# 98 transposes in pairs on the halves of the array, and the mLSTM's state products by head

## Chip, cores and metric

The kernel runs on one core of a Trainium2 chip. The metric is the device time of one execution in microseconds (us). The kernel before takes 916.1 us (median of 3 runs, 916.0 to 916.24); a change of about 0.2% (1.8 us) is what a measurement of this kernel can tell from no change.

## The reference

One decoder layer on x of 512 tokens by 1024 features, all float32: half a step of a gated FFN, a token mixer with two groups of heads, and a second FFN, each between RMS norms.

```python
x = x + 0.5 * rms_norm(swiglu_ffn(rms_norm(x, norm_pre[0]), ffn1_w_in, ffn1_w_out), norm_post[0])
x = x + rms_norm(token_mixer(rms_norm(x, norm_pre[1]), w_mix_in, ...), norm_post[1])
x = x + 0.5 * rms_norm(swiglu_ffn(rms_norm(x, norm_pre[2]), ffn2_w_in, ffn2_w_out), norm_post[2])

def swiglu_ffn(x, w_in, w_out):            # D_FF = 2816
    gate, up = split(x @ w_in, 2)
    return (silu(gate) * up) @ w_out

# token_mixer: one projection h @ w_mix_in gives all heads their inputs
#   HGRN2, 4 heads of 128:   S_t = diag(f_t) S_{t-1} + (1 - f_t) v_t^T,  o_t = S_t^T q_t
#   mLSTM, 4 heads, q and k of 64, v of 128:
#       num = inter * q.C + P.v,   den = inter * q.n + sum(P),   h = num / max(|den|, exp(-m))
#       C, n: a running state of k v^T and of k, decayed by the gates
#   each head normed and gated, both groups side by side, then @ w_mix_out
```

## The kernel before

**Products.** TensorE multiplies in float32r, with every operand as a high part and a low part, three products for one (`mm3`, lines 198 to 200; `prod`, line 619; `in_k`, line 549). So whatever is a factor is first "split": ScalarE casts the high part (line 370 for activations, 294 and 299 for weights), VectorE subtracts it from the source to get the low part (lines 371, 296, 302). `xq[0..3]` hold the activations in this form, features on the partitions: index 2c+h is token half c (256 tokens) and feature half h.

**Transposes.** Activations come with tokens on the partitions, so each tile i of 128 tokens is turned: `turn` (line 364) makes four 128x128 transposes into one PSUM bank, by a product with an identity as the moving operand and the tile as the weights. The bank is then evicted by one cast and one subtraction. `to_t` does this for both feature halves, `to_s` for tiles 0 and 1 of the second FFN (`part`, lines 384 and 386, which also keeps a copy, line 388), `hgrn_edges` for decayed keys of HGRN2 (line 1403), `mlstm_scores` for the keys of the mLSTM (line 1672). There are 146 such transposes; 48 at the head of both FFNs (`start`, `sums`) have no part in the change.

**mLSTM values.** `mlstm_values(c)` runs for the four chunks of 128 tokens. For each pair p of heads it takes a PSUM bank, multiplies the queries of both heads (2 x 64 rows) with a state `C` that is block diagonal (258 columns, zeros off the blocks; line 1739), and adds for each head P times v (line 1742, 129 columns: 128 values and the denominator). ScalarE squares from the bank (line 1747), VectorE and GpSimd work out a factor, VectorE writes the result (line 1761), and with that the bank is free. `chunks` runs three such chunks in a staggered way and fills in with `fill`, pieces of a running projection (lines 198 to 200).

**Order.** Each engine runs its instructions in one fixed order. Most of it is the order of the program text as the framework's scheduler rearranges it when the kernel is built; PSUM is a ring of eight banks, and a bank is handed out again when its last reader is done. Around the change: in `mix_out0` (the output projection's left half) all four tiles of the HGRN2 half of `y` are turned first and the first half of the products follows, then the mLSTM half tile by tile. In the second FFN's head (`ffn_head`), after the last product of the right half (`last`), product p1 (line 619, 24 matmuls over both token tiles 0 and 1: eight with high parts, eight with the low part of the activations, eight with the low part of the weights) starts at once.

Of the kernel before, what the change touches and what calls it, by code (L numbers as in the profile page):

```python
# [11 lines left out]
ALU = mybir.AluOpType  # L12
# [111 lines left out]
class Layer:  # L124
    def __init__(self, ctx, tc, aps):
        self.tc, self.nc = tc, tc.nc
        self.__dict__.update(aps)
        nc = self.nc
        pool = lambda name, **kw: ctx.enter_context(tc.tile_pool(name=name, bufs=1, **kw))
        self.cp, self.wp, self.sp, self.psp = pool("cp"), pool("wp"), pool("sp"), pool("psp", space=PSUM)  # L130
        self.uid, self.hold = 0, ()
        self.wt, self.free, self.slot = None, deque(), {}

        self.ident = self.cp.tile([P, P], F32, name="ident")
        make_identity(nc, self.ident)
# [4 lines left out]
        xq = {n: self.cp.tile([P, 2 * D + 2 * STEP * (n == 0)], F32R, name=f"xq{n}") for n in (1, 2, 3, 0)}  # L140
        self.xt = [xq[n] for n in range(4)]
        self.xq = [t[:, : 2 * D].rearrange("p (b k t) -> p b k t", b=2, k=KH) for t in self.xt]

        x0 = self.xt[0].rearrange("p (b x) -> p b x", b=2)[:, :, :D].rearrange("p b (k t) -> p b k t", k=KH)
        self.xh = [x0, *self.xq[1:]]
        self.prm = self.cp.tile([P, 36], F32, name="prm")
        self.dram = dram = ctx.enter_context(tc.tile_pool(name="sums", bufs=1, space=bass.MemoryType.DRAM))
        self.sums_of = {
            (f, h, k2): dram.tile([P, 4, QUARTER], F32, name=f"{f}sums{h}_{k2}")
            for f in ("f1", "f2") for h in range(2) for k2 in OUT[f][h] if k2 in QUARTERED[f][h]  # L150
        }
# [212 lines left out]
            self.nc.tensor.transpose(pt[:, c * P : (c + 1) * P], src[:, k * P : (k + 1) * P], self.ident)  # L364
        return pt.rearrange("p (c t) -> p c t", c=4)

    def two(self, dst, i, src):

        v = slice((i % 2) * P, (i % 2 + 1) * P)
        self.nc.scalar.copy(dst[:, 0, :, v], src)  # L370
        self.low = self.nc.vector.tensor_tensor(dst[:, 1, :, v], src, dst[:, 0, :, v].bitcast(F32), op=ALU.subtract)

    def to_t(self, i, src, halves=(0, 1)):

        for h in halves:
            self.two(self.xq[2 * (i // 2) + h], i, self.turn(src, h))

    def part(self, i, h, src):

        pv = self.turn(src, h)  # L380
        v = slice(i * P, (i + 1) * P)
        dst = self.xh[h][:, :, :, v]
        yield
        self.nc.scalar.copy(dst[:, 0], pv)
        yield
        self.nc.vector.tensor_tensor(dst[:, 1], pv, dst[:, 0].bitcast(F32), op=ALU.subtract)
        yield
        self.nc.scalar.copy(self.xf[h][:, :, v], pv)
        yield

    def sums(self, i, src):
# [1003 lines left out]
    def hgrn_edges(self, p, d):  # L1395

        nc = self.nc
        qd = self.qd[:, 2 * p : 2 * p + 2, :]
        nc.vector.tensor_tensor(qd, self.q[p][:, :, P:], qd, op=ALU.mult)
        for a in range(2):  # L1400
            pt = self.ps()
            for c in range(NT - 1):
                nc.tensor.transpose(pt[:, c * P : (c + 1) * P], d[:, a, c * P : (c + 1) * P], self.ident)
            nc.scalar.copy(self.kdt[:, 2 * p + a, :], pt[:, : 3 * P])

    def hgrn_level(self, p, n, ke):

# [229 lines left out]
    def mlstm_scores(self, mc):  # L1637
# [31 lines left out]
        turned = [self.ps() for _ in range(2)]  # L1669
        for p, pt in enumerate(turned):  # L1670
            for c in range(3):
                nc.tensor.transpose(pt[:, c * P : (c + 1) * P], self.qk[:, 2 + p, c * P : (c + 1) * P], self.ident)
        for p in range(2):
            wp = self.col(8)[:, :6]
            nc.vector.tensor_copy(wp.rearrange("p (c a) -> p c a", a=2), w[:, :3, 2 * p : 2 * p + 2])
            nc.vector.tensor_tensor(
                self.kw[:, p].rearrange("p c (a d) -> p (c a) d", a=2),
                turned[p][:, : 3 * P].rearrange("p (n d) -> p n d", d=64),
                wp[:, :, None].broadcast_to([P, 6, 64]),
                op=ALU.mult,  # L1680
            )
# [49 lines left out]
    def mlstm_values(self, c):  # L1731

        nc = self.nc
        s = slice(c * P, (c + 1) * P)
        pm = []
        for p in range(2):
            ps = self.ps()
            if c:
                nc.tensor.matmul(ps[:, :258], self.qdm[:, p, (c - 1) * P : c * P], self.C[:, p, c - 1, :], start=True, stop=False)  # L1739
            for a in range(2):  # L1740
                o = ps[:, 129 * a : 129 * a + 129]
                nc.tensor.matmul(o, self.pT[:, 2 * p + a, s], self.vm[:, c, 2 * p + a, :], start=c == 0, stop=c == 0 or a == 1)  # L1742
            pm.append(ps[:, :258].rearrange("p (a v) -> p a v", a=2))
        sq = self.sp.tile([P, 512], F32, tag="junk", bufs=1, name=self.nm("sq"))
        den, ab, ss, r = self.col(4), self.col(4), self.col(4), self.col(4)
        for p in range(2):
            nc.scalar.activation(sq[:, 256 * p : 256 * p + 256].rearrange("p (a v) -> p a v", a=2), pm[p][:, :, :P], AF.Square)
        yield
        for p in range(2):
            nc.vector.tensor_copy(den[:, 2 * p : 2 * p + 2].rearrange("p (a o) -> p a o", o=1), pm[p][:, :, P : P + 1])  # L1750
# [6 lines left out]
        f = self.rpow(ss, 1.0 / P, EPS)  # L1757
        nc.gpsimd.tensor_tensor(f, f, r, op=ALU.mult)
        yield
        for p in range(2):  # L1760
            nc.vector.tensor_tensor(
                self.y[:, c, W + 256 * p : W + 256 * p + 256].rearrange("p (a v) -> p a v", a=2),
                pm[p][:, :, :P],
                f[:, 2 * p : 2 * p + 2].rearrange("p (a o) -> p a o", o=1).broadcast_to([P, 2, P]),
                op=ALU.mult,
            )
        yield

    def chunks(self, make, n):
# [8 lines left out]
    def mixer(self):  # L1778
# [3 lines left out]
        with tc.tile_pool(name="ma", bufs=1) as ma:  # L1782
# [35 lines left out]
            with tc.tile_pool(name="mc", bufs=1) as mc:  # L1818
# [28 lines left out]
    def mix_out0(self):  # L1847
# [130 lines left out]
```

## Time and profile before

| | us |
|---|---|
| median of 3 runs | 916.1 (916.0 to 916.24) |
| the profiled execution | 916.13 |
| its span in the profile | 914.4 |
| mean granted TensorE clock | 0.999 of full speed |
| VectorE busy | 767.2 |
| ScalarE busy | 522.0 |
| GpSimd busy | 183.7 |

How to read it: times are us from the span's start. A row of the timeline has start, duration, engine, line, operation, output and inputs, shapes, and the count of instructions in the row. The duration of a matmul holds a modelled tail, so one starts long before the record of the one before it ends; the step is what counts, the distance from start to start. A matmul whose duration is longer than that of its like was issued early and waited by the difference. PEld is the loading of weights, which runs beside the matmul before it. Products of plain float32 are recorded as two passes.

### The profile page before, as it was taken

The page shows a single profiled execution, that of the slowest core. Times are in us where ns is not written, and L with a number is a line of the kernel's source. Part 1 is how long each engine was busy: PE and PEld are TensorE (multiplying, and loading weights), DVE is VectorE, ACT ScalarE, POOL GpSimd, SP SyncE. Part 2 cuts the span into 40 slices and gives each one's busy share as a digit, 9 for nine tenths or more (in the row PEclk, how much of TensorE's full clock was granted, in tenths as well). Part 3 has the DMA queues.
Part 4 walks back from the last instruction along what each step waited for, and adds up shares of the span by engine and source line. Part 5 has one row for each costly group of instructions (what it writes and reads, how often), then busy time and mean ns, then how long its engine had stood idle before and what let it go on. Part 6 is the DMA issues. An engine that isn't in the chain of part 4 may idle for free.

```text
span 914.4 us, 18150 instructions
## 1 busy us (share of the span) xinstructions
PE 906.1 (99%) x7330; PEld 874.9 (96%) x7330; DVE 767.2 (84%) x1005; ACT 522.0 (57%) x749; POOL 183.7 (20%) x256
## 2 busy tenths in 40 slices
PE   9999999999999999999999999999999999999997
PEld 8999999999999999998888887899999999999997
DVE  6899988889888876799896556799999889998886
ACT  7645545557566567957643345684454545757661
POOL 2541112121111047742230300322000000010002
PEclk9999999999999999999999999999999999999999
DMA  9355779775897815898953126253344445378542
GB/s 306 88 165 136 189 188 216 187 159 138 219 280 233 258 55 144 162 192 207 214 112 109 47 70 213 65 161 102 97 148 139 138 123 159 104 231 246 170 146 93
DMA packets 127921, 146.51 MB, mean 160 GB/s; under 512 B 16335, under 2 KB 100303, under 8 KB 127837
## 3 DMA queue, kind: packets, MB, share of 16 engines
q1 hardware_dynamic: 111868, 130.14, 46.4%
q0 software_dynamic: 15680, 14.69, 11.9%
q8 instruction: 57, 0.93, 0.4%
q10 hardware_dynamic: 288, 0.52, 0.2%
q14 instruction: 28, 0.22, 0.1%
HBM read 143.20 MB, written 31.48 MB: 191 GB/s over the span
## 4 chain that ended last, share of the span: by engine, by line
PE 62%; ACT 0%; DVE 0%; DVEq 0%; POOLq 0%; issue 0%; POOL 0%; ACTq 0%
PE ps L619 23%; PE ps L1012 8%; PE ps L549 6%; PE ps L198 5%; PE ps L200 5%; PE ps L199 5%; PE ps L1004 4%; PE ps L560 1%; PE ps L1441 1%; PE ps L364 1%; PE ps L1540 0%; PE ps L1742 0%; PE ps L1491 0%; PE ps L1715 0%; PE ps L1739 0%; PE ps L1717 0%
## 5 line engine op out<-in xcount | busy, mean ns | idle before, releaser
L294 ACT CAST w<-raw 128x1024 fp32r<-128x1024 f32 x246 | 250.6, 1027 | 192.0 <-PE ps L619 91.1
L296 DVE TENSOR_TENSOR w<-raw,w 128x1024 fp32r<-128x1024 f32 x246 | 299.4, 1221 | 30.3 <-ACT w L294 28.9
L619 PE MATMUL ps<-xq,w 128*128 128x256 f32 x2016 | 237.4, 277 | 0.0
L619 PEld LDWEIGHTS ps<-xq,w 128*128 128x128 f32 x2016 | 233.3, 188 | 0.1
L619 PE MATMUL ps<-sq,w 128*128 128x256 f32 x1512 | 178.0, 276 | 0.0
L619 PEld LDWEIGHTS ps<-sq,w 128*128 128x128 f32 x1512 | 174.6, 188 | 0.0
L310 DVE TENSOR_TENSOR raw<-raw,raw 128x1024 f32<-128x1024 f32 x72 | 89.7, 1252 | 7.5 <-DMA raw<-in_ffn_w_in_dram 6.2
L1012 PE MATMUL ps<-w,hs 128*128 128x256 f32 x672 | 80.9, 276 | 0.0
L1004 PE MATMUL ps<-w,hs 128*128 128x256 f32 x672 | 79.2, 276 | 0.0
L1012 PEld LDWEIGHTS ps<-w,hs 128*128 128x128 f32 x672 | 78.3, 188 | 0.0
L1004 PEld LDWEIGHTS ps<-w,hs 128*128 128x128 f32 x672 | 77.5, 188 | 0.0
L198 PE MATMUL ps<-w,xq 128*128 128x512 f32 x176 | 71.1, 405 | 0.1
L199 PE MATMUL ps<-w,xq 128*128 128x512 f32 x176 | 68.6, 391 | 0.0
L200 PE MATMUL ps<-w,xq 128*128 128x512 f32 x176 | 68.6, 391 | 0.0
L549 PE MATMUL ps<-xq,w 128*128 128x256 f32 x480 | 55.7, 277 | 0.0
L944 POOL DMA_DIRECT2D f2sums<-in_ffn_w_out_dram x15 | 20.0, 1507 | 177.5 <-DMA f2sums<-in_ffn_w_out_dram 177.0
L549 PEld LDWEIGHTS ps<-xq,w 128*128 128x128 f32 x480 | 54.9, 188 | 0.5 <-issue 0.5
L884 ACT CAST hs<-hf 128x1024 fp32r<-128x1024 f32 x32 | 33.7, 1054 | 28.0 <-PE ps L1012 20.3
L885 DVE TENSOR_TENSOR hs<-hf,hs 128x1024 fp32r<-128x1024 f32 x32 | 39.1, 1223 | 9.0 <-ACT hs L884 8.4
L944 POOL DMA_DIRECT2D f1sums<-f1sums x26 | 22.3, 859 | 110.1 <-DMA f1sums<-in_ffn_w_out_dram 56.1
L944 POOL DMA_DIRECT2D f2sums<-f2sums x30 | 26.3, 905 | 87.1 <-DMA f2sums<-in_ffn_w_out_dram 42.4
L310 POOL TENSOR_TENSOR raw<-raw,raw 128x1024 f32<-128x1024 f32 x12 | 32.6, 2724 | 40.9 <-DVE w L296 40.7
(263 smaller groups left out, 1232.9 us busy)
## 6 DMA issues: line engine op xcount, KB each, us to landing
raw<-in_ffn_w_in_dram SPq DMA_DIRECT2D x98, 512.0 KB, 4.7
raw<-in_ffn_w_out_dram SPq DMA_DIRECT2D x44, 512.0 KB, 5.1
raw<-in_w_mix_in_dram SPq DMA_DIRECT2D x28, 512.0 KB, 5.7
raw<-f2sums SPq DMA_DIRECT2D x15, 512.0 KB, 5.2
raw<-f1sums SPq DMA_DIRECT2D x13, 512.0 KB, 7.0
raw<-in_w_mix_out_dram SPq DMA_DIRECT2D x8, 512.0 KB, 4.3
f2sums<-in_ffn_w_out_dram SPq DMA_DIRECT2D x30, 128.0 KB, 5.0
f2sums<-in_ffn_w_out_dram SPq DMA_DIRECT2D x15, 256.0 KB, 6.1
```

The costliest lines, as they stand in the source:

```text
L198: mm(ps, sh, mh, start=start, stop=False, **kw)
L199: mm(ps, sh, ml, start=False, stop=False, **kw)
L200: mm(ps, sl, mh, start=False, stop=stop, **kw)
L294: nc.scalar.copy(hi, raw)
L296: self.low = nc.vector.tensor_tensor(lo, raw, hi.bitcast(F32), op=ALU.subtract)
L310: added = (nc.vector if late else nc.gpsimd).tensor_tensor(o, o, c, op=ALU.add)
L549: mm(ps[:, u0:u1], w[:, a, k, :], self.xop(k, b, u0, u1), start=k + n + m == 0, stop=k == ND - 1 and n == 2, skip_group_check=True,)
L619: self.nc.tensor.matmul(ps[:, c], wb[b][:, k, v], left[d][:, k, :], start=first and a + n + k == 0, stop=n == 2 and k == KH - 1, skip_grou ...
L885: self.nc.vector.tensor_tensor(lo, src, hi.bitcast(F32), op=ALU.subtract)
L944: nc.gpsimd.dma_start(to[:, a:b], v, accum_op=ALU.add)
L1004: mm(out, a[kk][:, i * P : (i + 1) * P], w[:, b, kk, QUARTER * v : QUARTER * (v + 1)], start=begin and c == kk == n == 0, stop=kk == 1 and ...
L1012: mm(ps[:, QUARTER * c : QUARTER * (c + 1)], A[a][:, c], B[b], start=begin and c == n == 0, stop=n == 2, skip_group_check=True,)
```

## The change

1. `turns` replaces `turn` at 98 places: each 128x128 transpose becomes two with 64 rows (64 tokens) each, one on rows 0 to 63 of the array and one on rows 64 to 127. The moving identity has 64 columns and not 128. The two go to two PSUM banks, so that a bank holds one half of the tokens of all the tiles turned. Eight transposes that filled one bank after the other become eight pairs which fill two banks together.
2. The evictions stay as many and as large (512 columns), but each covers 64 tokens of every block and not 128 tokens of half the blocks. For this `xq` becomes one tile, with the same places inside.
3. In `mix_out0` two token tiles are turned together (`to_t2`).
4. In `mlstm_values` the product with the state is made by head, on 64 rows and 129 columns, the two heads of a pair on the two halves of the array, and the banks are by row half a and no longer by pair p. Both banks are taken ahead of the first product.

```diff
+    def turns(self, srcs):
+        pts = [self.ps() for _ in range(2)]
+        for n, src in enumerate(srcs):
+            for u, pt in enumerate(pts):
+                r = slice(64 * u, 64 * u + 64)
+                self.nc.tensor.transpose(pt[:, 64 * n : 64 * n + 64], src[r], self.ident[r, r])
+        return [pt[:, : 64 * len(srcs)] for pt in pts]
...
+    def parts(self, hi, lo, src):
+        self.nc.scalar.copy(hi, src)
+        self.low = self.nc.vector.tensor_tensor(lo, src, hi.bitcast(F32), op=ALU.subtract)
...
-    def to_t(self, i, src, halves=(0, 1)):
-        for h in halves:
-            self.two(self.xq[2 * (i // 2) + h], i, self.turn(src, h))
+    def to_t(self, i, src):
+        x = self.xq[2 * (i // 2) : 2 * (i // 2) + 2]
+        for u, pt in enumerate(self.turns(self.tiles(src, ND))):
+            hi, lo = (self.pair(*(t[:, b, :, self.at(i, u)] for t in x)) for b in range(2))
+            self.parts(hi, lo, pt.rearrange("p (h k t) -> p h k t", h=2, t=64))
+    def to_t2(self, i, h, srcs):
+        x = self.xq[2 * (i // 2) + h]
+        for u, pt in enumerate(self.turns([t for src in srcs for t in self.tiles(src)])):
+            hi, lo = (self.pair(*(x[:, b, :, self.at(c, u)] for c in range(2))) for b in range(2))
+            self.parts(hi, lo, pt.rearrange("p (c k t) -> p c k t", c=2, t=64))
...
     def to_s(self, i, src):
         if i < 2:
-            for h in range(2):
-                g = self.part(i, h, src)
-                for _ in range(3):
-                    next(g)
+            for u, pt in enumerate(self.turns(self.tiles(src, ND))):
+                g = self.part2(i, u, pt)
+                next(g)
                 self.copies.append(g)
...
-        for p in range(2):
-            ps = self.ps()
-            if c:
-                nc.tensor.matmul(ps[:, :258], self.qdm[:, p, (c - 1) * P : c * P], self.C[:, p, c - 1, :], start=True, stop=False)
-            for a in range(2):
-                o = ps[:, 129 * a : 129 * a + 129]
-                nc.tensor.matmul(o, self.pT[:, 2 * p + a, s], self.vm[:, c, 2 * p + a, :], start=c == 0, stop=c == 0 or a == 1)
+        banks = [self.ps()[:, :258].rearrange("p (q v) -> p q v", q=2) for _ in range(2)]
+        for p in range(2 * (c > 0)):
+            for a, ps in enumerate(banks):
+                r, t, v = slice(64 * a, 64 * a + 64), slice((c - 1) * P, c * P), slice(129 * a, 129 * a + 129)
+                nc.tensor.matmul(
+                    ps[:, p], self.qdm[r, p, t], self.C[r, p, c - 1, v], start=p == 0, stop=False, skip_group_check=True
+                )
+        for a, ps in enumerate(banks):
+            for p in range(2):
+                nc.tensor.matmul(
+                    ps[:, p], self.pT[:, 2 * p + a, s], self.vm[:, c, 2 * p + a, :], start=c == p == 0, stop=p == 1,
+                    skip_group_check=True,
+                )
...
-                for i in range(NT):
-                    self.to_t(i, self.y[:, i], (0,))
+                for i in (0, 2):
+                    self.to_t2(i, 0, [self.y[:, i + n, :W] for n in range(2)])
...
-                if part:
-                    self.to_t(i, self.y[:, i], (1,))
+                if part and i % 2 == 0:
+                    self.to_t2(i, 1, [self.y[:, i + n, W:] for n in range(2)])
```

The order of instructions moves at three places that matter below. A row has the line, the operation, output and inputs with buffer numbers, the shape, a count, and in brackets the engines waited for.

TensorE, chunk 2 of the mLSTM values, before: the products with the state (line 1739) and with v (line 1742), and the projection on both sides.

```order
L200 MATMUL ps_5675<-w,xq_75 128x512
L1739 MATMUL ps_5930<-C,qdm 128x258 [waits Activation_49]
L1742 MATMUL ps_5930<-vm,pT 128x129 x2
L1739 MATMUL ps_5934<-C,qdm 128x258 [waits DVE_49,PE_49]
L1742 MATMUL ps_5934<-vm,pT 128x129 x2
L198 MATMUL ps_5676<-w,xq_77 128x512
```

The same place now (lines 1773 and 1778):

```order
L200 MATMUL ps_5716<-w,xq 128x512
L1773 MATMUL ps_5979<-C,qdm 128x129 [waits Activation_49]
L1773 MATMUL ps_5980<-C,qdm 128x129 [waits DVE_49,PE_49]
L1773 MATMUL ps_5979<-C,qdm 128x129
L1773 MATMUL ps_5980<-C,qdm 128x129
L1778 MATMUL ps_5979<-vm,pT 128x129 x2
L1778 MATMUL ps_5980<-vm,pT 128x129 x2
L198 MATMUL ps_5717<-w,xq 128x512
```

The wait for VectorE, which releases the second bank (chunk 0's first), stood behind one product with the state and two with v; it stands behind one short product now.

ScalarE at the start of the output projection, before: `mo` is the last gate of the mLSTM half, `xq<-ps` are the casts of the four turned tiles, `w<-raw` casts halves of weight slabs.

```order
L1843 ACTIVATE mo_6217<-ps_6007 128x512
L370 CAST xq_78<-ps_6220 128x4x128
L370 CAST xq_78<-ps_6227 128x4x128
L370 CAST xq_76<-ps_6234 128x4x128
L370 CAST xq_76<-ps_6241 128x4x128
L299 ACTIVATE w<-raw_6087,prm 128x512
```

The same place now:

```order
L1877 ACTIVATE mo_6270<-ps_6060 128x512
L299 ACTIVATE w<-raw_6140,prm 128x512
L384 CAST xq<-ps_6273 128x2x4x64
L384 CAST xq<-ps_6274 128x2x4x64
L384 CAST xq<-ps_6295 128x2x4x64
L384 CAST xq<-ps_6296 128x2x4x64
```

The weight cast has moved from behind the four casts of `xq` to ahead of them; and the first two of these now make up tiles 0 and 1 together, where each made one tile.

VectorE ahead of the second FFN's first product, before: `xq<-ps` (line 386) are the low parts of tile 0 (two rows) and of tile 1 (two rows), `xn` is the norm of tile 2, `ps<-ps` and `xs` belong to the residual.

```order
L509 SCALAR_TENSOR_TENSOR xs<-ps_6433,col_6588,xs 128x512
L386 TENSOR_TENSOR xq_78<-ps_6607,xq_78 128x4x128
L386 TENSOR_TENSOR xq_75<-ps_6614,xq_75 128x4x128
L481 SCALAR_TENSOR_TENSOR xn_6604<-xs,col_6602,gpre_6493 128x512 x2
L386 TENSOR_TENSOR xq_78<-ps_6633,xq_78 128x4x128
L386 TENSOR_TENSOR xq_75<-ps_6640,xq_75 128x4x128
L501 TENSOR_TENSOR ps_6434<-ps_6434,gpost_6248 128x512
```

The same place now:

```order
L546 SCALAR_TENSOR_TENSOR xs<-ps_6518,col_6673,xs 128x512
L424 TENSOR_TENSOR xq<-ps_6692,xq 128x2x4x64
L518 SCALAR_TENSOR_TENSOR xn_6689<-xs,col_6687,gpre_6578 128x512 x2
L424 TENSOR_TENSOR xq<-ps_6693,xq 128x2x4x64
L424 TENSOR_TENSOR xq<-ps_6726,xq 128x2x4x64
L424 TENSOR_TENSOR xq<-ps_6727,xq 128x2x4x64
L538 TENSOR_TENSOR ps_6519<-ps_6519,gpost_6317 128x512
```

One low part of tile 0 has moved behind the norm of tile 2. Before, a row held one feature half of a tile (`xq_78` is `xq[0]`, the one that p1 reads); now each holds both feature halves of 64 tokens, so p1 needs all four. On every engine the rest of the order is the same but for a few exchanges of neighbours.

More of the change, by code (lines that the diff above doesn't have):

```diff
@@ L138, in __init__ @@
         self.xs = self.cp.tile([P, NT, D], F32, name="xs")
-        xq = {n: self.cp.tile([P, 2 * D + 2 * STEP * (n == 0)], F32R, name=f"xq{n}") for n in (1, 2, 3, 0)}
-        self.xt = [xq[n] for n in range(4)]
+        xq = self.cp.tile([P, 8 * D + 2 * STEP], F32R, name="xq")
+        self.xt = [xq[:, 2 * D * o : 2 * D * (o + 1) + 2 * STEP * (o == 3)] for o in (3, 0, 1, 2)]
         self.xq = [t[:, : 2 * D].rearrange("p (b k t) -> p b k t", b=2, k=KH) for t in self.xt]
@@ L388, in part, with part2 @@
         self.nc.scalar.copy(self.xf[h][:, :, v], pv)
+        yield
+    def part2(self, i, u, pt):
+        pv = pt.rearrange("p (h k t) -> p h k t", h=2, t=64)
+        v = self.at(i, u)
+        hi, lo = (self.pair(*(self.xh[h][:, b, :, v] for h in range(2))) for b in range(2))
+        self.nc.scalar.copy(hi, pv)
+        self.nc.vector.tensor_tensor(lo, pv, hi.bitcast(F32), op=ALU.subtract)
+        yield
+        self.nc.scalar.copy(self.pair(*(x[:, :, v] for x in self.xf)), pv)
         yield
@@ L1399, in hgrn_edges @@
         nc.vector.tensor_tensor(qd, self.q[p][:, :, P:], qd, op=ALU.mult)
-        for a in range(2):
[L1401 to L1404, printed above, removed]
+        for u, pt in enumerate(self.turns([t for a in range(2) for t in self.tiles(d[:, a], NT - 1)])):
+            kd = self.kdt[:, 2 * p : 2 * p + 2, :].rearrange("p a (c k) -> p a c k", c=3)[:, :, :, 64 * u : 64 * u + 64]
+            nc.scalar.copy(kd, pt.rearrange("p (a c k) -> p a c k", a=2, c=3))
     def hgrn_level(self, p, n, ke):
@@ L1759, in mlstm_values @@
         yield
[L1760 to L1766, printed above, removed]
+        for ps, out, g in zip(banks, heads(self.y[:, c, W:]), heads(f)):
+            nc.vector.tensor_tensor(out, ps[:, :, :P], g.broadcast_to([P, 2, P]), op=ALU.mult)
         yield
```

37 lines of the change are left out of this document (18 added, 19 removed).

## The prediction

> **What bounds the kernel now.** First the page's busy times.
>
> ```profile
> span 914.4 us, 18150 instructions
> PE 906.1 (99%) x7330; PEld 874.9 (96%) x7330; DVE 767.2 (84%) x1005; ACT 522.0 (57%) x749; POOL 183.7 (20%) x256
> ```
>
> TensorE is never without work, so a step saved on it comes off the end, unless it runs into a wait; and a new wait of TensorE is added in full. The profiled execution took 916.13 us, 1.7 more than its span and level with the median of 916.1; sums below are made against 916.13. Next the chain of work, for what a transpose costs between products.
>
> ```profile
> 344.52 0.87 PE ps L364 x8
> ...
> 351.83 32.64 PE ps L549 x288
> ```
>
> Eight transposes take 0.87, 109 ns each; a 256-column product takes 113 ns. The 98 transposes thus hold TensorE for 10.7 us, the most that could be won.
>
> **What a half transpose costs.** The trace has no 64-row transpose, but it has products on halves of the array: the scores on row halves (line 1632) and the state updates on column halves (line 1693), between projection products (whose step is 0.227; the rows in (f) show two in sequence, 0.39 long and overlapping).
>
> ```profile
> 478.20 1.16 PE L1632 MATMUL ps<-qk 64*128 64x128 f32 x16
> 479.29 0.50 PE L198 MATMUL ps<-w,xq 128*128 128x512 f32 x1
> ...
> 489.30 0.39 PE L200 MATMUL ps<-w,xq 128*128 128x512 f32 x1
> 489.62 1.10 PE L1693 MATMUL ps<-vm,kw 128*64 128x129 f32 x16
> 490.65 0.50 PE L198 MATMUL ps<-w,xq 128*128 128x512 f32 x1
> ...
> 491.91 0.40 PE L200 MATMUL ps<-w,xq 128*128 128x512 f32 x1
> 492.24 0.66 PE L1693 MATMUL ps<-vm,kw 128*64 128x129 f32 x8
> 492.83 0.50 PE L198 MATMUL ps<-w,xq 128*128 128x512 f32 x1
> ```
>
> Eight records more (16 against 8) cost 1.10 - 0.66 = 0.44, so 55 ns each, 0.11 for two: two halves run side by side in the time of one. The rest is the price of going to halves and back. The L198 behind lasts 0.50 and not 0.39, so it begins 0.11 late. From the L200 ahead to it: 490.76 - 489.30 - 0.227 = 1.23, less 8 x 0.11 = 0.35; and 492.94 - 491.91 - 0.227 = 0.80, less 4 x 0.11 = 0.36. **Going in and out costs 0.36.** The transposes' weights load as fast as these:
>
> ```profile
> L364 PEld LDWEIGHTS ps<-ident,y 128*128 128x128 f32 x32 | 3.7, 140 | 0.4
> ...
> L1693 PEld LDWEIGHTS ps<-vm,kw 128*64 128x64 f32 x24 | 1.3, 136 | 0.7 <-DVE C L1704 0.4 <-issue 0.4
> ```
>
> (140 against 136 ns), so I take the same 0.36. How the step falls with columns:
>
> ```profile
> 403.53 1.78 PE ps L1441 x16
> ...
> 498.13 0.43 PE ps L1739 x2
> ```
>
> 128 columns take 111 ns, 258 take 215: 0.8 ns a column, so 64 columns save 51 of the 109 to 111. I take **59 ns for a pair**. Below, 53 if the whole cost were by column; above, 111, if no step can fall under the 55 ns per record that the trace shows at its shortest. The trace cannot exclude the upper end.
>
> **The sum, group by group.** n transposes held 0.109n; n pairs hold 0.059n + 0.36.
>
> (a) Tiles 0 and 1 ahead of the mixer, 8 each: 0.87 becomes 0.83. What follows waits for ScalarE:
>
> ```profile
> 337.79 0.95 ACT w L294
> 338.79 5.73 PE ps L560 x48
> ```
>
> L560 starts when the weight cast ends, which hangs on ScalarE's own queue. Gain 0.
>
> (b) Tiles 2 and 3: 2 x (0.83 - 0.87) = -0.08. (c) `hgrn_edges`, 6 each, twice: 0.71 for 0.65, **+0.12**; a small group doesn't pay for its two switches.
>
> (d) The mLSTM's keys stand right behind scores that are on halves already.
>
> ```profile
> 483.60 1.16 PE L1632 MATMUL ps<-qk 64*128 64x128 f32 x16
> 484.69 0.87 PE L1672 MATMUL ps<-ident,qk 128*128 128x128 f32 x6
> 485.32 0.47 PE L198 MATMUL ps<-w,xq 128*128 128x512 f32 x1
> ```
>
> From the scores' start to the L198's real one (485.32 + 0.08) were 1.80; without transposes (the other group above) 479.40 - 478.20 = 1.20. With six pairs in the same mode 1.20 + 6 x 0.059 = 1.55: **-0.25**.
>
> (e) mLSTM values. In each of chunks 1 to 3 two state products of 0.43 (row above) become four pair steps of 0.11, plus 0.36 and some 0.04 for longer weights: 0.84 for 0.86, -0.02 for each of chunks 1 and 3. Chunk 2 waits:
>
> ```profile
> 501.13 0.59 PE L1739 MATMUL ps<-C,qdm 128*128 128x258 f32 x2
> ...
> 501.69 0.76 DVE L1761 TENSOR_TENSOR y<-ps,col 128x256 f32<-128x256 f32 x2 [1.73 <-POOL col L1758]
> ...
> 502.26 0.67 PE L1739 MATMUL ps<-C,qdm 128*128 128x258 f32 x2
> ...
> 503.13 0.47 PE L198 MATMUL ps<-w,xq 128*128 128x512 f32 x1
> ```
>
> Its second bank is chunk 0's first, free when the first of the two L1761 is done, about 502.1; that one waited for GpSimd's factor and comes no sooner. The second L1739 started at 502.26 + 0.08 = 502.34 (0.67 for 0.59). Before, 0.88 of work stood ahead of this wait; now one short product. TensorE waits from about 501.5 to 502.34, then has four passes of the second half (0.44), the way out (0.2) and eight passes with v (0.89): the next L198 at 503.87, before 503.13 + 0.08. **+0.66**.
>
> (f) First half of the output projection.
>
> ```profile
> 535.41 0.73 ACT L299 ACTIVATE w<-raw,prm 128x512 fp32r<-128x512 f32 x1
> 536.15 0.60 ACT L1843 ACTIVATE mo<-ps 128x512 f32<-128x512 f32 x1
> 536.65 2.05 ACT L370 CAST xq<-ps 128x512 fp32r<-128x512 f32 x4
> ...
> 535.44 0.39 PE L199 MATMUL ps<-w,xq 128*128 128x512 f32 x1
> 535.66 0.39 PE L200 MATMUL ps<-w,xq 128*128 128x512 f32 x1
> ...
> 538.18 0.50 PE L200 MATMUL ps<-w,xq 128*128 128x512 f32 x1
> ```
>
> Before, from the L200 ahead to the third product's real start (538.29) 2.63 went by, less three steps 1.95. Now TensorE would be ready at 537.2 (535.66 + 0.23 + 16 x 0.059 + 0.36), but ScalarE runs the weight cast first (0.73, as in the row), then the casts: from 537.3, 0.5 each, two done at 538.37. Two are needed for tile 0, as each holds 64 tokens. With 0.14 until a product starts (below, 550.15 to 550.30): 538.51, so 2.62 are lost, and 0.07 more at tile 2, for cast 4. 2.69 - 1.95 = **+0.74**. VectorE subtracts the weight's low part by 538.2 and then 0.62 each (h), two by 539.4; L200 comes at 539.9, since the high parts of tiles 0 to 2 go first.
>
> (g) Second half.
>
> ```profile
> 549.57 1.05 ACT L370 CAST xq<-ps 128x512 fp32r<-128x512 f32 x2
> ...
> 548.51 0.39 PE L200 MATMUL ps<-w,xq 128*128 128x512 f32 x1
> ...
> 550.19 0.50 PE L198 MATMUL ps<-w,xq 128*128 128x512 f32 x1
> ...
> 558.38 0.39 PE L200 MATMUL ps<-w,xq 128*128 128x512 f32 x1
> ...
> 558.96 0.47 PE L198 MATMUL ps<-w,xq 128*128 128x512 f32 x1
> ...
> 559.73 0.85 PE L198 MATMUL ps<-w,xq 128*128 128x512 f32 x2
> ```
>
> Before: 1.56 to the first product, 0.13 for a single transpose between, 0.43 around the last four, 0.23 wait in the last row (0.85 for 0.62): 2.35. Now all sixteen pairs come at once and are done by 550.0; the first product waits for two casts, to 550.65, and starts at 550.79: 2.05. **-0.30**.
>
> (h) Head of the second FFN.
>
> ```profile
> 584.47 1.41 DVE L481 SCALAR_TENSOR_TENSOR xn<-xs,col,gpre 128x512 f32<-128x512 f32 x2 [0.86 <-POOL col L458]
> 585.80 1.28 DVE L386 TENSOR_TENSOR xq<-ps,xq 128x512 fp32r<-128x512 f32 x2
> ...
> 585.76 2.99 PE L619 MATMUL ps<-xq,sq 128*128 128x256 f32 x24
> ```
>
> The ninth matmul of L619 (585.76 + 8 x 0.118 = 586.70, the step being 2.99 less a tail of 0.28 over 23) is the first to read a low part; it needed the first of the two L386, done halfway, at about 586.5. Now three subtractions stand behind the norm of tile 2, which still waits for GpSimd, and all are needed: 585.80 + 3 x 0.62 = 587.7, matmul at 587.85. **+1.15**. The gain of tiles 0 and 1 goes into this wait. I count nothing behind it: TensorE comes later, and the engines that feed it gain that time. Exchanges of neighbours on ScalarE, VectorE and SP's queue around 430 us touch weight slabs split some products ahead; I cost them at nothing too, and each would be one more wait if that cover were gone.
>
> Sum: -0.08 + 0.12 - 0.25 + 0.62 + 0.74 - 0.30 + 1.15 = **+2.0: 918.1 us**. Of the array's own gain little is left, since each group pays 0.36; what is lost are three waits, two for evictions and one for a bank. I cost evictions with 64-column rows as before (same count, same 512 columns): the trace has no such rows; bounds none and 0.1 each.
>
> [...] The 55 ns per record are the row. [...]
>
> **Rivals.** *Pairs no shorter than 0.11* (halves at 55 ns per record; the change then does not do what it is for): 34 pairs stand where nothing hides them (16 of b, 12 of c, 6 of d), 34 x 52 ns = +1.8: 919.9. For it: no shorter step in the trace; against it: the step follows the columns. *No switch within transposes*: the 0.36 was read at products, and if a transpose could enter without it, b, c, d and e would win 0.36 x 4, 0.2 and 0.4 x 2, some 2.4 in all: 915.7, not slower. It decides by the switch: under 0.07 the time is that of before, over 0.33 it is slower by more than 0.2%; against it: both halves, rows and columns, show the same price. *The low part is not late*: if (h) doesn't appear, since the norm of tile 2 comes sooner, 917.0. For it: that norm hangs on a chain over three engines; against: the chain begins at a product that hasn't moved. *Slower evictions*, 0.1 more each, in f, g and h, 7 in a row on the path: 918.8.
>
> **How the numbers follow.** Forecast 0.45, with 0.5 to either side, mostly above 917.9, 0.3 slower and 0.15 within. Pairs no shorter 0.15, slower evictions 0.1: slower. No late low part 0.15: within. No switch 0.15: 0.1 within, 0.05 faster. In all faster 0.05, within 0.2% (1.8 us, what a measurement can tell) 0.4, slower 0.55. The range leaves out half of the no-switch case and the tail above: 915.7 to 920.0.
>
> **What would show it.** Pairs at 59 ns; 0.36 around each group; TensorE waiting about 0.85 in chunk 2 for L1761's like, 1.3 for the casts in f, 1.2 at the ninth matmul of p1. It is wrong if the step of pairs or the switch differs, or if one of these waits isn't there or another is.

## The result

The changed kernel takes 922.19 us (median of 4 runs, 921.34 to 924.66), the kernel before 916.05 beside it: ratio 1.0073, interval 1.0053 to 1.0093. It is slower by 6.1 us; the forecast was 2.0 slower, and 922.19 lies above its range. The profiled execution took 921.34, the fastest of the four.

### The profile after

The page of the kernel after, first its busy times, then the first product group of the second FFN and the casts and subtractions of its operand, with the idle time ahead of them and what ended it.

```profile
span 919.6 us, 18372 instructions
PE 905.7 (98%) x7440; PEld 872.0 (95%) x7440; DVE 769.3 (84%) x1005; ACT 522.8 (57%) x749; POOL 184.3 (20%) x256
...
L656 PE MATMUL ps<-xq,sq 128*128 128x256 f32 x192 | 25.1, 292 | 3.4 <-ACT xq L423 3.0 <-ACT xq L411 0.4
L424 DVE TENSOR_TENSOR xq<-ps,xq 128x512 fp32r<-128x512 f32 x4 | 2.8, 688 | 1.7 <-ACT xq L423 1.7
L423 ACT CAST xq<-ps 128x512 fp32r<-128x512 f32 x4 | 2.3, 580 | 3.8 <-DVE xq L424 3.8
```

TensorE was busy for 906.1 of 914.4 before and is busy for 905.7 of 919.6 now: its idle time has grown from 8.3 to 13.9. 3.0 of that is one wait for a cast, and the casts waited 3.8 for VectorE's subtractions. No step of the prediction has casts that wait for VectorE.

Where the time goes is best read by matching the starts of all products that both traces have and following how far the later ones lag. The lag grows and shrinks at these places only:

| | forecast | in the trace |
|---|---|---|
| start of the kernel, before any changed line | 0 | +0.49 |
| (a) tiles 0 and 1 ahead of the mixer | 0 | -0.02 |
| (b) tiles 2 and 3 | -0.08 | -0.19 |
| (c) `hgrn_edges`, twice | +0.12 | +0.14, and +0.20 behind the first |
| (d) keys of the mLSTM | -0.25 | -0.26 |
| (e) values of the mLSTM | +0.62 | +0.61 |
| (f) first half of the output projection | +0.74 | +0.74 |
| (g) its second half | -0.30 | -0.42 |
| (h) head of the second FFN | +1.15 | -0.07 for its transposes, +3.20, then +1.62 |
| the rest of the second FFN | 0 | -0.87 |

The last column sums to the 5.2 by which the span grew. The start is no effect of the change: another execution of the same kernel (e11) stands at -0.11 there, so later lags are given without it. The terms (a) to (g) are within 0.12 of the forecast, but for the 0.20 behind (c). (h) is off by 3.6; of what else was not foreseen, +0.49 and +0.20 stand against -0.87, and that they nearly cancel is luck.

**Pairs and switch.** The timeline of the kernel after, first a group of 16 pairs, then one of 8 between products:

```profile
536.65 0.39 PE L200 MATMUL ps<-w,xq 128*128 128x512 f32 x1
536.97 1.21 PE L373 MATMUL ps<-ident,y 64*128 64x64 f32 x32
539.36 0.50 PE L198 MATMUL ps<-w,xq 128*128 128x512 f32 x1 [1.18 <-ACT xq L384]
...
579.56 0.39 PE L200 MATMUL ps<-w,xq 128*128 128x512 f32 x1
579.88 0.72 PE L373 MATMUL ps<-ident,xn 64*128 64x64 f32 x16
580.52 0.50 PE L198 MATMUL ps<-w,xq 128*128 128x512 f32 x1
```

Eight pairs more cost 1.21 - 0.72 = 0.49: 61 ns a pair (forecast 59). From the L200 to the next product's real start (0.50 for 0.39, so 0.11 late) are 580.63 - 579.56 - 0.227 = 0.84, less 8 x 0.061: the switch is 0.35 (forecast 0.36). In the group of 16 the L198 starts at 539.47, 2.82 after the L200 (forecast 538.51 - 535.66 = 2.85), behind the casts.

**The head of the second FFN.** ScalarE, then VectorE and TensorE, in the timeline of the kernel after:

```profile
580.65 0.58 ACT L423 CAST xq<-ps 128x512 fp32r<-128x512 f32 x1
584.57 0.57 ACT L423 CAST xq<-ps 128x512 fp32r<-128x512 f32 x1
587.87 0.59 ACT L423 CAST xq<-ps 128x512 fp32r<-128x512 f32 x1 [2.73 <-DVE xq L424]
589.55 0.59 ACT L423 CAST xq<-ps 128x512 fp32r<-128x512 f32 x1 [1.09 <-DVE xq L424]
...
583.62 0.68 DVE L424 TENSOR_TENSOR xq<-ps,xq 128x512 fp32r<-128x512 f32 x1
585.76 1.42 DVE L518 SCALAR_TENSOR_TENSOR xn<-xs,col,gpre 128x512 f32<-128x512 f32 x2 [1.46 <-POOL col L495]
587.09 0.69 DVE L424 TENSOR_TENSOR xq<-ps,xq 128x512 fp32r<-128x512 f32 x1
588.49 0.69 DVE L424 TENSOR_TENSOR xq<-ps,xq 128x512 fp32r<-128x512 f32 x1 [0.71 <-ACT xq L423]
...
586.76 0.39 PE L200 MATMUL ps<-w,xq 128*128 128x512 f32 x1
590.18 4.61 PE L656 MATMUL ps<-xq,sq 128*128 128x256 f32 x24 [3.04 <-ACT xq L423]
```

Read the casts from the third on: each begins 0.1 to 0.4 after the subtraction of the cast before it has ended (587.09 + 0.69, then 588.49 + 0.69), and the third subtraction in turn waits for its own cast. The norm of tile 2 (585.76) stands on VectorE ahead of the second subtraction, so the norm holds up casts as well as low parts. TensorE starts its first product at 590.18, when the fourth cast is done; it never gets to wait at the ninth. Second, the 24 products last 4.61, where they lasted 2.99 before.

### The profile page after: what moved, and what is told of

It is laid out like the page before. It is cut to its first block, busy times and chain, and to the rows that moved or that the text cites. A ratio compares the mean times of both kernels' runs of the same rounds, so it can differ in the third digit from the quotient of the medians.

```text
span 919.6 us, 18372 instructions
## 1 busy us (share of the span) xinstructions
PE 905.7 (98%) x7440; PEld 872.0 (95%) x7440; DVE 769.3 (84%) x1005; ACT 522.8 (57%) x749; POOL 184.3 (20%) x256
## 4 chain that ended last, share of the span: by engine, by line
PE 60%; ACT 1%; DVE 1%; POOL 0%; issue 0%; DVEq 0%; POOLq 0%; ACTq 0%
PE ps L656 23%; PE ps L1049 8%; PE ps L586 6%; PE ps L198 5%; PE ps L200 4%; PE ps L199 4%; PE ps L1041 4%; PE ps L597 1%; PE ps L1476 1%; PE ps L1575 0%; PE ps L1526 0%; PE ps L1749 0%; ACT junk L490 0%; PE ps L373 0%; PE ps L1751 0%
## 5 line engine op out<-in xcount | busy, mean ns | idle before, releaser
L198 PE MATMUL ps<-w,xq 128*128 128x512 f32 x176 | 71.2, 405 | 1.8 <-ACT xq L384 1.8
L200 PE MATMUL ps<-w,xq 128*128 128x512 f32 x176 | 68.3, 391 | 0.0
L198 PEld LDWEIGHTS ps<-w,xq 128*128 128x128 f32 x176 | 33.1, 188 | 9.5 <-ACT xq L384 2.3
```

What stands on the lines that cost most here:

```text
L198: mm(ps, sh, mh, start=start, stop=False, **kw)
L200: mm(ps, sl, mh, start=False, stop=stop, **kw)
```

## The experiments

Each is set beside runs of the kernel before on the same chip (median 915.6 to 915.8 in the three sets). Theory A has two parts: the casts wait for VectorE by a dependency that the data do not have, and the idle time behind it lowers TensorE's clock. The rivals are slower evictions, and a loss that sits elsewhere.

### e1: equal distances

The first cast's rows and the next subtraction's touch no common element. But `pair` describes the two feature halves of a split as one access with a large stride, and `x0` keeps its two blocks 16 elements further apart than the others. The four casts as the program has them on ScalarE, with the engines waited for, after the change and then with the edit:

```
L423 CAST xq<-ps_6692 128x2x4x64 [waits PE_49]
L423 CAST xq<-ps_6693 128x2x4x64 [waits DVE_49,PE_49]
L423 CAST xq<-ps_6726 128x2x4x64 [waits DVE_49,PE_49]
L423 CAST xq<-ps_6727 128x2x4x64 [waits DVE_49,PE_49]

L423 CAST xq<-ps_6692 128x2x4x64 [waits PE_49]
L423 CAST xq<-ps_6693 128x2x4x64 [waits PE_49]
L423 CAST xq<-ps_6726 128x2x4x64 [waits PE_49]
L423 CAST xq<-ps_6727 128x2x4x64 [waits PE_49]
```

```diff
-        self.xh = [x0, *self.xq[1:]]
+        self.xh = self.xq
```

> The second block of the first operand tile moves 16 elements, so that both blocks of both halves lie at the same distance; nothing is left out. Theory A (most of the miss is one wait ahead of the second FFN: each cast of its operand waits for VectorE's subtraction of the cast before, since the program orders overlapping address ranges, and the two blocks' unequal distances make them seem to overlap): the casts wait for TensorE alone, two subtractions instead of four hang behind the norm, the ninth product waits some 0.5 us as worked out for two low parts (587.2 against 586.7), the clock stays full, and of the 4.8 us that the head of the second FFN lost some 0.5 stay: 917.9, by 0.3 either way. Rival B (the evictions with 64-column rows, or the number of low parts behind the norm, make the wait): the wait stays over 1 us, 918.5 to 922.

916.28 us (12 runs; before 915.7; ratio 1.0034, 1.0006 to 1.0061). The timeline of e1, ScalarE, VectorE and TensorE:

```profile
580.12 1.07 ACT L423 CAST xq<-ps 128x512 fp32r<-128x512 f32 x2
584.05 1.05 ACT L423 CAST xq<-ps 128x512 fp32r<-128x512 f32 x2
...
586.58 1.28 DVE L424 TENSOR_TENSOR xq<-ps,xq 128x512 fp32r<-128x512 f32 x2
...
586.46 1.10 PE L656 MATMUL ps<-xq,sq 128*128 128x256 f32 x8
587.91 2.16 PE L656 MATMUL ps<-xq,sq 128*128 128x256 f32 x16 [0.35 <-DVE xq L424]
```

The casts run two by two behind TensorE, the first eight products start at once, and the ninth waits for the low parts, as the prediction's step (h) has it, with two subtractions behind the norm instead of three. The lag of this stage is 0.63 in place of 4.8 (expected 0.5). The median is 5.9 under that of the first comparison, beyond the expected 4.3; the rest may be the lower clock of three of those four runs (e11) and the stretches described at the end, which was not tried. Four of its 12 runs took 922.0 to 927.4 at the same clock, which no other kernel's runs show; they widen the interval, and their cause is open.

### e3: the head of the second FFN as before

```diff
-            for u, pt in enumerate(self.turns(self.tiles(src, ND))):
-                g = self.part2(i, u, pt)
-                next(g)
+            for h in range(2):
+                g = self.part(i, h, src)
+                for _ in range(3):
+                    next(g)
```

> The eviction and the transposes ahead of the second FFN (tiles 0 and 1) as in the kernel before, the rest as changed; nothing is left out. Theory A: all 4.8 us at the head of the second FFN go, and the 0.03 that each of the two groups of transposes gained are lost: 922.2 - 4.8 + 0.07 = 917.5. Rival B (the loss comes from the groups ahead, or TensorE meets another wait there): 918.5 or more.

917.18 us (11 runs; ratio 1.0014, 1.0006 to 1.0023). In its trace the lag grows by 0.06 at this place. All of the 4.8 is tied to `to_s`, the time is 0.3 under the expected 917.5, and the other terms stand.

### e8: the halves one after the other

```diff
-        for n, src in enumerate(srcs):
-            for u, pt in enumerate(pts):
+        for u, pt in enumerate(pts):
+            for n, src in enumerate(srcs):
```

> In each group all transposes of the lower row half come first, then all of the upper one; nothing else changes. Theory A (a pair is as short as one half because the two halves run side by side, which needs neighbours on different halves): each record then takes about 60 ns, a group of 8 pairs 0.96 us in place of 0.50 and of 16 pairs 1.9 in place of 0.98. Rival B (the shorter step comes of the 64 columns alone): about 31 ns a record, as now.

One run, 921.93. The timeline of e8, a group of 16 pairs, one of 8, and the first product of the second FFN:

```profile
538.05 1.63 PE L373 MATMUL ps<-ident,y 64*128 64x64 f32 x32
...
581.91 1.02 PE L373 MATMUL ps<-ident,xn 64*128 64x64 f32 x16
...
592.24 3.06 PE L656 MATMUL ps<-xq,sq 128*128 128x256 f32 x24 [2.47 <-ACT xq L423]
```

The groups are longer by 0.30 and 0.42 than in pairs (0.72 and 1.21), so the 64 columns alone are not the reason that pairs are short. But 0.96 and 1.9 were expected of records that never overlap. In the group of 8 the trace, read by single records, has four steps of about 62 ns, then three times two records 6 to 8 ns apart (in the pairs of the kernel after 3 to 4, with 62 from pair to pair), then steps of 62 again. Which record is which can be told from one of them: the last transpose of the first half, the eighth in the program, is the one that signals that its bank is full, and in the trace it is the eleventh to start. So three of the second half have started ahead of it, beside the first half's last ones. Five of the eight pairs then take two steps instead of one, 5 x 0.061 = 0.30, as measured (in the group of 16, seven of the pairs, 0.43 for 0.42); the rest of the bad order costs nothing.

### e2 and e9: work in the wait

```diff
+        if self.second and not self.had:
+            for n in range(28):
+                self.nc.tensor.matmul(ps[:, :HALF], wb[1][:, n % KH, :P], wb[0][:, n % KH, :], start=True, stop=True, skip_group_check=True)
```

In e9 the range is 6.

> 28 products of ready weights are added into the accumulator ahead of the first product of the second FFN (which clears it), to keep TensorE at work through its 3.3 us wait; 28 x 0.113 = 3.2 us. Theory A (the half clock that follows the wait comes of TensorE's idleness): the granted clock stays 1.0, the 24 products behind take 2.8 us instead of 4.6, and the time is 922.2 - 1.5 = 920.7. Rival B (the low clock comes of something else, such as the work that starts there): the low stretch stays, 922.2 or more.

921.77 us (4 runs; ratio 1.0064, 1.0049 to 1.0078). TensorE in the timeline of e2:

```profile
586.85 3.51 PE L654 MATMUL ps<-sq 128*128 128x256 f32 x28
590.20 2.96 PE L659 MATMUL ps<-xq,sq 128*128 128x256 f32 x24
```

The same 24 products take 2.96 and not 4.61, at a granted clock of 1.00 (590 to 593), so the half clock is gone: 1.46 us were won by 590. But the total is hardly lower. The added products made the scheduler exchange pieces of work on ScalarE and VectorE behind that point, TensorE waits there (1.38 us from one product to the next at 611), and by 640 the 1.5 us are lost again. So the time was no test; the 24 products were.

> The changed kernel with only 6 instead of 28 added products ahead of the second FFN (0.68 us of work into an accumulator that the first real product clears), which leaves the order on ScalarE and VectorE nearly as it was. The wait ends when it did, but TensorE's longest gap between two starts is 3.43 - 0.68 = 2.75 us instead of 3.43. Theory A (a gap of 3.43 us brought the half clock, one of 2.86 us, as the halves in turn had it, does not; the 28 added products lost their gain again through another order of work behind them): full clock, the 24 products behind take 2.9 us instead of 4.6, and the time is 922.2 - 1.5 = 920.7. Rival B (the clock drops by something else than the gap): the half clock stays and the time is 922 or more.

920.99 us (4 runs, 920.01 to 921.49). The profiled execution, with a gap of only 2.61 between two starts, shows the half clock all the same, at a lag like that of the kernel after:

```profile
587.02 0.87 PE L654 MATMUL ps<-sq 128*128 128x256 f32 x6
590.22 4.60 PE L659 MATMUL ps<-xq,sq 128*128 128x256 f32 x24 [2.33 <-ACT xq L423]
```

Theory A as it stood (a gap of some 3 us lowers the clock) falls: 2.61 did here, and 2.86 did not in e8 (24 products in 3.06). The clock's records in the trace of the kernel after are: from 7.05 full for 583.679, half for 3.413 (590.73 to 594.14), full for 324.266, then half to the end, behind the last product. In the kernel before it is full for 907.945. The three full stretches are 171, 95 and 266 times 3.4133, the drop between them is one. From these lengths comes the author's guess: the clock is set for stretches of a fixed grid, by what the stretch before held. The windows of the kernel after and of e9 by that grid, its edges read from the drop in each (busy time of PE and its instructions, PEld, DVE, ACT, POOL, then the granted clock):

```profile
587.30:590.70 3.40, 0.52 (x4) 0.52 (x5) 1.71 (x3) 1.74 (x5) 0.00 (x0) 1.00 0.01 2
590.70:594.10 3.40, 3.40 (x18) 3.40 (x18) 3.11 (x5) 2.38 (x7) 1.50 (x3) 0.50 0.00 0
594.10:597.50 3.40, 3.40 (x31) 3.40 (x30) 2.07 (x4) 3.40 (x8) 1.25 (x4) 0.99 0.57 156
```

```profile
587.20:590.60 3.40, 1.07 (x9) 0.87 (x9) 1.71 (x4) 1.60 (x4) 0.00 (x0) 1.00 0.01 2
590.60:594.00 3.40, 3.40 (x19) 3.40 (x18) 3.11 (x5) 2.38 (x7) 1.36 (x3) 0.50 0.00 0
```

The stretch that follows one with 0.52 or 1.07 of work runs at 0.50: 18 or 19 products in place of 31. Whether the grid decides, and not the length of the wait, was then tried with the changed kernel alone.

### e11: the changed kernel again

> The changed kernel itself once more, for the spread of its times against the mean granted clock of each run. Theory A (the clock is set for stretches of 3.41 us on a grid of its own, and one stretch at half clock, 1.6 us, follows where TensorE's 3 us wait fills most of one): runs with a mean clock of 0.998 to 0.999, where the wait falls across two stretches, take about 920.4; with 0.996 to 0.997 (one low stretch more: 3.41 x 0.5 of 920 is 0.0019) 921.5 to 922; with 0.994 to 0.995 (two) 923 or more. Rival B (time and clock have nothing to do with each other): the times of these groups overlap.

920.83 us (5 runs). In order of time: 919.94 at a mean clock of 0.999, 920.37 at 0.998, then 920.83, 920.87 and 921.39 at 0.997; the first four runs had 921.34 at 0.997 and 921.90, 922.49 and 924.66 at 0.994. Over these nine runs a lower clock goes with a longer time, without exception, so the rival falls; but the sizes are not those expected (the runs at 0.997 lie under 921.5, and two of the three at 0.994 under 923). The runs at 0.994 have no trace, so what else ran at half clock there is open. The profiled one of the five, 920.37, has the same wait and the full clock:

```profile
589.61 3.05 PE L656 MATMUL ps<-xq,sq 128*128 128x256 f32 x24 [3.04 <-ACT xq L423]
```

No change of its clock marks the edges of the grid here. Counted on from the clock's first record, which is an estimate, they let the wait fall across two stretches:

```profile
584.40:587.80 3.40, 2.17 (x10) 1.46 (x8) 2.01 (x3) 0.67 (x2) 0.67 (x2) 1.00 0.00 0
587.80:591.20 3.40, 1.59 (x13) 1.59 (x14) 2.00 (x4) 2.20 (x5) 0.82 (x2) 1.00 0.01 2
591.20:594.60 3.40, 3.40 (x32) 3.40 (x31) 2.53 (x3) 2.49 (x7) 1.57 (x3) 1.00 0.00 0
```

Same kernel, same wait of 3.04, and 32 products in the next stretch instead of 18. Its lag behind the kernel before is 4.05 at 590, that of the first profile 5.58: one low stretch costs 1.53 at this place. The end of the run does not show all of it: at 666 e11 has a wait of TensorE for VectorE that the first profile does not have, and it adds 1.09 to the lag. VectorE had waited 3.39 and not 1.76 for a weight transfer at 649, and has no idle time from there to 666. The first profile, then e11:

```profile
649.51 1.22 DVE L310 TENSOR_TENSOR raw<-raw,raw 128x1024 f32<-128x1024 f32 x1 [1.76 <-DMA raw<-in_ffn_w_in_dram]
```

```profile
649.02 1.23 DVE L310 TENSOR_TENSOR raw<-raw,raw 128x1024 f32<-128x1024 f32 x1 [3.39 <-DMA raw<-in_ffn_w_in_dram]
...
666.44 1.76 PE L656 MATMUL ps<-sq,w 128*128 128x256 f32 x13 [0.86 <-DVE ps L675]
```

### e6: the first half of the output projection as before

On e3's kernel, so that the head of the second FFN is out of the way.

```diff
-                for i in (0, 2):
-                    self.to_t2(i, 0, [self.y[:, i + n, :W] for n in range(2)])
+                for i in range(NT):
+                    self.two(self.xq[2 * (i // 2)], i, self.turn(self.y[:, i], 0))
```

> On the kernel with the head of the second FFN as before: also the first half of the output projection's operand as before, four full transposes and an eviction for each tile, in the order of before; nothing is left out. Theory A (the 1.40 us from the last transpose to the first product come of the weight cast ahead of the casts and of two casts needed): the gap falls to about 0.2 to 0.3, the low part's wait of 0.18 comes back, and this stage gives back 0.74: 917.2 - 0.7 = 916.4, by 0.5 for TensorE's stretches of longer steps. Rival B (the gap comes of the way out of the halves, not of the casts): the stage gains under 0.4.

916.44 us (10 runs, ratio 1.0010, 1.0000 to 1.0019), 0.74 under e3; the two intervals overlap, so the trace decides. Its timeline:

```profile
536.30 1.91 PE L364 MATMUL ps<-ident,y 128*128 128x128 f32 x16
537.97 0.48 PE L198 MATMUL ps<-w,xq 128*128 128x512 f32 x1
```

The transposes take longer (1.91 for 1.21), and the first product comes sooner. The lag grows by 0.00 in this stage, by 0.74 in e3, so term (f) belongs to this edit. The edit takes back the switch, the order and the two casts together; which of them it is shows in the trace of the kernel after, where the pairs end at 538.2 and the first product waits 1.18 longer, for the second cast. So it is the weight cast and the two casts, and not the switch.

### e10: products with v ahead of the wait

On e3's kernel; `own(a, ...)` is the loop over p of products with v for bank a.

```diff
+        own(0, True, c == 0)
         for p in range(2 * (c > 0)):
...
-        for a, ps in enumerate(banks):
-            for p in range(2):
+        own(1, c == 0, True)
```

> On the kernel with the head of the second FFN as before: the mLSTM's products with v for the lower heads' bank go ahead of the four pairs on the row halves, those for the other bank behind; nothing is left out. Theory A (TensorE's 0.85 us in chunk 2 is the wait for the second bank): 0.45 of work moves ahead of the wait, the gap falls from 0.85 to about 0.4, and 0.45 is won: 916.7, by 0.5. Rival B (the wait is for the first bank, or for the change of halves itself): the gap stays, and the time with it.

917.26 us (10 runs), not to be told from e3; the trace decides. Chunk 2 in the timeline of the kernel after, then of e10:

```profile
501.58 0.49 PE L1773 MATMUL ps<-C,qdm 64*128 64x129 f32 x2
502.65 0.68 PE L1773 MATMUL ps<-C,qdm 64*128 64x129 f32 x6 [0.58 <-DVE y L1800]
```

```profile
501.19 0.61 PE L1773 MATMUL ps<-vm,pT 128*128 128x129 f32 x4
501.72 0.49 PE L1781 MATMUL ps<-C,qdm 64*128 64x129 f32 x2
502.36 0.68 PE L1781 MATMUL ps<-C,qdm 64*128 64x129 f32 x6 [0.15 <-DVE y L1804]
```

The wait for the bank falls from 0.58 to 0.15, as much as the work moved ahead of it, and what the chunk adds to the lag from 0.68 to 0.25. Term (e) is this wait, as forecast; the time of the whole is too coarse for 0.45.

### e5 and e12: only what pays

Changed are (a), (b), (d) and (g); `to_s`, `hgrn_edges`, `mlstm_values` and the first half of the output projection are as before.

> Only the groups that gained in the trace are changed: tiles 0 to 3 ahead of the mixer, the mLSTM's keys behind the scores, and the second half of the output projection; the rest is as before, and nothing is left out. Theory A (the groups' prices add up as read from the trace, 62 ns a pair and 0.35 a group): ahead of the mixer -0.2, keys -0.26, second half -0.45: 0.9 faster than before, 915.2 against 916.05. Rival B (what TensorE gains there it loses at the next wait for ScalarE or VectorE): within 0.3 of before.

> The kernel with only the paying groups changed once more, for a narrower interval. Theory A: 0.84 us were won at the head of the second FFN in the trace; 915.6 - 0.84 = 914.8, ratio 0.999. Rival B (nothing is won): ratio 1.000.

915.03 us (11 runs; ratio 0.9995, 0.9986 to 1.0004) and again 914.76 (11 runs; ratio 0.9991, 0.9982 to 1.0000). In both traces the lag behind the kernel before is -0.84 at the head of the second FFN: -0.16, -0.26 and -0.42 in (b), (d) and (g). So the gain shows in both traces, and the medians lie 0.6 and 1.0 under those of the kernel before; by the intervals it is about a tenth of a per cent, barely told from none. It has the lowest median here.

## Why the prediction was right and wrong

**Right.** TensorE is the bound, and single terms add up along it. The price of a pair (61 for 59 ns) and of the switch (0.35 for 0.36) hold, though the trace of before had neither on transposes: they were read from products on halves. (d), (e) and (f) came within 0.01, with the waits where the prediction put them: 0.85 from start to start in chunk 2, and the first half's product 2.82 after its L200 (2.85). Of the rivals, pairs no shorter than 0.11, no switch and a low part in time are refuted by these rows, and slower evictions by the means: with rows of 64 columns the subtractions take 688 ns and the casts 580, against 682 and 590 before in the rows of the same place:

```profile
L386 DVE TENSOR_TENSOR xq<-ps,xq 128x512 fp32r<-128x512 f32 x8 | 5.2, 682 | 0.3 <-ACT xq L384 0.3
...
L384 ACT CAST xq<-ps 128x512 fp32r<-128x512 f32 x8 | 4.3, 590 | 1.1 <-PE ps L364 1.1
```

**Wrong: step (h).** It said that all three late subtractions are needed at the ninth product, at 587.7, and took the casts as done. It looked at how the order had changed on VectorE and did not ask why the scheduler had put one subtraction and three casts later, nor what the four casts wait for in the changed program. The wait that decided stands there: three of four casts wait for VectorE. Casts and subtractions became one chain over two engines, with the norm of tile 2 in it, and the first product had to wait, not the ninth. With that dependency gone (e1), the wait at the ninth product appears, for two subtractions instead of three: 0.63, not 1.15. The wait at the first product is 3.20, less the 1.15 of the forecast and the 0.07 that the transposes gained: 2.0 of the 3.6 missed.

**Wrong: "a new wait of TensorE is added in full".** It is added in full, and then once more in part: in the profiled run the 3.2 us of waiting brought 1.62 us at half clock behind it, the other part of the 3.6. It was not weighed at all that a wait can cost more than its length. Whether it does changes from run to run: three of the four runs of the first comparison have a mean clock of 0.994, none of e11's five is under 0.997, and the median of the first is 1.4 longer.

**Sizes.** (g) gained 0.12 more than forecast: the stage after stands as forecast (the first product starts 2.30 after the L200, 2.28 in the forecast), but the stage before had lost another 0.10 to a later wait that the sum left out. (b) gained 0.11 more, because some 30 products between its two groups have steps of 118 ns in the kernel before and of 113 now. (c) cost 0.20 more, because the 48 products behind its first group, from 406 to 411 us, have 118 now and had 113 before. That is the change's doing, as far as these traces go: e1, e3 and e6 have the 0.20 too, and neither e5 and e12, where (c) is undone, nor e8 have it; why is open. The exchanges around 430 us, costed at nothing, cost nothing: the lag stands still from 411 us to the second group of (c). The rest of the second FFN gave 0.87 back: that is a stretch of such long steps in the profile of the kernel before, not a gain of the change.

## What to carry over

When the built order shows a helper instruction moved back, ask which dependency moved it, and read the waits of the changed program on the engine that feeds the critical one: an access that spans two far blocks with unequal distances can tie engines together that share no data (three of four casts waited for VectorE here, and none in e1). Price a short kernel change by groups: halving the rows saved 48 ns a transpose but cost 0.35 us to enter and leave, so groups of eight gain next to nothing, and what decides is which wait ends last behind them. Behind TensorE's waits of 3.21 and 2.50 us the next 24 products took 4.61 and 4.60, behind those of 3.22 and 2.65 (e11, e8) 3.05 and 3.06: a forecast with a new wait of that length should carry a second term of some 1.5 us, with a chance.

## What was not expected of the hardware

- **The granted clock was halved for 3.413 us behind some waits and not behind others.** It was behind the wait of 3.21 us in the kernel after and that of 2.50 in e9; it was not behind 3.22 in e11 and 2.65 in e8. By a grid of 3.413 us, 2.87 of the 3.21 fell into one stretch (84% of it), and all of the 2.50 (73%); the 3.22 were split into 42% and 53%, the 2.65 into 27% and 50%. The shares are estimates, from the ends of the products and the grid, whose edges in e11 and e8 are counted on from the first record of the clock. These four cases are all there are; if the share decides, the limit lies between 53% and 73% by them. The same program was 1.53 us apart behind such a wait.
- **Halves overlapped that are not neighbours in the program**: in the group of 8 of e8 three transposes of the second half start ahead of the first half's last (0.30 longer for 8 pairs, where 0.46 were expected).
- **Products of 256 columns had two steps**, 113 and 118 ns, at a granted clock of 1.00, and stayed in one for a while (medians of the steps in the kernel before: 113 from 670 to 690 us, 118 from 692 to 709). The windows of the kernel before show it (busy time of line 619's products, their count, granted clock, DMA share and GB/s): 172 in 20 us between 178 and 179.

```profile
670.00:690.00 20.00, 20.00 (x178) 1.00 0.41 131
692.00:712.00 20.00, 20.00 (x172) 1.00 0.50 159
715.00:735.00 20.00, 20.00 (x179) 1.00 0.38 116
```

  This stretch began behind a product that was held up by 0.06 and cost 0.8 in all. Other traces have such stretches elsewhere: e3 two, of 169 and 288 products, some 2 us, e1 none in the second FFN. Why one begins or ends was not tried. More traffic of transfers alone is not the cause: the kernel after has as much as this stretch, 159 GB/s, and the short step.

```profile
670.00:690.00 20.00, 20.00 (x178) 1.00 0.52 159
```

  Together with waits like that of e11 at 666 (e2, e6 and e10 have one there too, between 0.4 and 0.8 in lag) it can make single times of one kernel differ by 1 to 2 us, as an estimate from these numbers, and so terms under 0.5 were read from the traces.
